# First modulation: shift and scale of the first eight k-tiles together on TensorE, without GpSimd

## The chip, the cores and the metric

The kernel runs on one core of a Trainium2 chip. The metric is the device time of one execution in microseconds (us); lower is better. Each kernel is run several times, and its median counts. One execution was also taken by the hardware profiler, and all rows below come from that one.

## What is computed

Two transformer blocks on 256 tokens of width 2048 in float32. The part at issue is the very start of the first block: a modulation of the latent `x` and of the context `ctx`, each by its own condition, and the projection of both to keys and values.

```python
def modulation(cond, w, b, n):
    m = jax.nn.silu(cond) @ w[:, :n * D_MODEL] + b[:n * D_MODEL]
    return jnp.split(m, n, axis=-1)
...
        sh, sc, gt = modulation(c_lat, w_ada[i], b_ada[i], 3)
        u = x * (1.0 + sc) + sh
...
                sh_c, sc_c = modulation(c_c, w_ada[i], b_ada[i], 2)
                uc = ctx_s * (1.0 + sc_c) + sh_c
                s_f, s_b = context_states(uc @ w_in_e[j][:, :E_STATE_COLS], w_gate_f[j], b_gate_f[j],
                                          w_gate_b[j], b_gate_b[j])
```

`w_ada[0]` is 2048 x 6144: its first 2048 columns give the shift, the next 2048 the scale. Both conditions (latent and context) meet the same weights, so the product has two rows only. Element k of shift and scale is needed before column k of `x` can enter the product `u @ w_in_e`.

## The kernel before

**Split products.** Every large product is done in three passes. `load_w` (line 157) brings two k-tiles of weights, 128 x 2 x 512 floats or 512 KB, into a buffer `wr` (four of them) by a DMA from the SP queue. `split_w` casts them to `wh` on ScalarE (line 148; three buffers) and subtracts, `wl = wr - wh`, one k-tile at a time (line 154; three buffers) on the engines of `split_on`: at first `(V, G)`, so that the first k-tile goes to VectorE and the second to GpSimd, from part 2 on `(V, V)`. `mm3` (lines 163 to 165) then does `wh*xh`, `wl*xh` and `wh*xl`. The `wr` buffer is free when the subtraction has read it.

**Modulation.** The 16 k-tiles of shift and scale are made in five parts, `PARTS = ((0, 2), (2, 2), (4, 4), (8, 4), (12, 4))` (first k-tile, count). The shift of a part (`ada_block`, kind 0) is made on TensorE: its weights go through `wr`, `wh`, `wl` like all others, and `c4`, the split condition with only four columns, is the stationary operand (lines 325 and 326). The four rows are copied (line 329), turned and summed by small products with `sel4` (line 332) and added to the bias in `mod0` (line 337). The scale of a part (`ada_block_v`, kind 1) is made on VectorE: its weights come into buffers `ar` (two of 256 KB), and each piece is multiplied by a column of the condition and added to `am`, once for the latent and once for the context (line 353 for the first, line 355 for the rest); products with a column of ones (line 361) sum over the partitions.

**Stages.** (A) The keys and values of the cross attention (`project(memT, ...)`, two blocks of 512 columns, eight steps each); beside it, in the background iterator `bg`, modulation part 0. (B) For each part j: transposes of `x` and `ctx` (line 234), scale and shift (`store_affine`, lines 249 to 252), and the products with `w_in_e` in four blocks of 512 columns, for two tiles of tokens of the latent and two of the context; beside it, in `bg`, modulation part j + 1. Part 0 leaves its sums in `kl`, `kc`, `vl`, `vc` by a copy on ScalarE (line 528). Later parts add to them: on VectorE straight from the accumulator (line 534), but for the odd tiles of tokens in parts 1 and 2 by a copy to `part` on ScalarE (line 531) and an addition on GpSimd (line 532).

**Order.** The engines run their queues in order. A scheduler of the framework sets the order of each queue from the program; work of `bg` can be moved ahead of where it is written when its buffers are free. DMAs go out from the SP queue in order, too: one that waits for its buffer holds up all behind it.

Of the kernel before, what the change touches and what calls it, by code (L numbers as in the profile page):

```python
# [17 lines left out]
D = 2048  # L18
# [36 lines left out]
def tile_kernel(ctx: ExitStack, tc: tile.TileContext, I: dict, out: bass.AP):  # L55
# [87 lines left out]
    split_on = [(V, G)]  # L143
# [26 lines left out]
    class XT:  # L170
        """x transposed, in two parts: pieces of four k-tiles, [128, 4, 256] each."""
# [10 lines left out]
    def project(x, w, c0, ncols, evac, korder=None, cw=512, w_k0=0, cbs=None, feed=None, lead=2, late=0, early=0):  # L182
        """evac(cb, t, acc) for each block of columns and each tile of tokens; feed makes x, two k-tiles at a step.
        late: the first tile of tokens is finished so many steps before the second, in the last block;
        early: the second is begun so many steps after the first, in the first block."""
# [43 lines left out]
    # transposes of two k-tiles for all tokens: src(t, kt) gives [128 tokens, 128]  # L229
# [13 lines left out]
    def store_affine(x, kt, pt, scale, bias, ts=(0, 1), scratch="h"):  # L243
        """scale(kt), bias(kt): columns [128, 1]."""
# [9 lines left out]
    def affine_steps(x, src, scale, bias, scratch="h"):  # L254
        """x from src, two k-tiles at a step; the first four k-tiles tile by tile of tokens."""
        for ts, kts in (((0,), (0, 2)), ((1,), (0, 2)), ((0, 1), range(4, 16, 2))):
            for kt in kts:
                store_affine(x, kt, transpose2(src, kt, ts), scale, bias, ts, scratch)
                yield

    # (v * scale + eps)^-1/2: a first guess from the bits, then Newton; v: [128, n]
# [22 lines left out]
    # the same for one column: a first guess by log and exp, of v * 2^-46 to stay in the log's range, then Newton  # L284
# [28 lines left out]
    mod0 = const([128, 16, 2, 2], "mod0")       # k-tile, (shift, 1 + scale), (latent, context)  # L313
    mod1 = const([128, 2, 16], "mod1")          # layer 1: (shift, 1 + scale), k-tile
    ada = [I["w_ada"][l] for l in range(2)]

    def ada_block(t0, nt, kind):
        """columns of modulation for the k-tiles t0 to t0 + nt, latent and context, on the tensor engine."""
# [15 lines left out]

    def set_mod0(pm, t0, nt, kind):
# [4 lines left out]
    def ada_block_v(t0, nt, kind):  # L340
        """the same on the vector engine."""
# [1494 lines left out]
```

## Time and profile before

| | |
|---|---|
| median of 3 runs | 2662.31 us (2661.46 to 2678.67) |
| profiled execution, its span | 2664.4 us, 2.1 us above that median |
| TensorE (PE) busy | 2522.0 us, 95% of the span |
| VectorE (DVE) busy | 1814.0 us, 68% |
| ScalarE (ACT) busy | 1164.6 us, 44% |
| GpSimd (POOL) busy | 260.0 us, 10% |
| DMA | 483.20 MB, 181 GB/s over the span |

The span runs from the first to the last instruction of the profiled execution. An engine's busy time counts its instructions, not what it waits. For TensorE it is modelled from pipelined products and says more than the product count: where a stage is dense, its products start 0.23 us apart though each shows 0.39 us. PEclk is the granted TensorE clock as a share of 2.4 GHz. A time "idle before" names what ended a wait.

### The profile page before, as it was taken

The page shows a single profiled execution, that of the slowest core. Times are in us where ns is not written, and L with a number is a line of the kernel's source. Part 1 is how long each engine was busy: PE and PEld are TensorE (multiplying, and loading weights), DVE is VectorE, ACT ScalarE, POOL GpSimd, SP SyncE. Part 2 cuts the span into 40 slices and gives each one's busy share as a digit, 9 for nine tenths or more (in the row PEclk, how much of TensorE's full clock was granted, in tenths as well). Part 3 has the DMA queues.
Part 4 walks back from the last instruction along what each step waited for, and adds up shares of the span by engine and source line. Part 5 has one row for each costly group of instructions (what it writes and reads, how often), then busy time and mean ns, then how long its engine had stood idle before and what let it go on. Part 6 is the DMA issues. An engine that isn't in the chain of part 4 may idle for free.

```text
span 2664.4 us, 33688 instructions
## 1 busy us (share of the span) xinstructions
PE 2522.0 (95%) x12095; PEld 2046.6 (77%) x12095; DVE 1814.0 (68%) x2960; ACT 1164.6 (44%) x1552; POOL 260.0 (10%) x213
## 2 busy tenths in 40 slices
PE   7889999889889899998999999999999999999998
PEld 5667866778677777787789778878788888888886
DVE  6799757897997877768656776675655544455544
ACT  5433244444654544436512352254554433444433
POOL 4430000220230000002010110100000000000000
PEclk9989999999999999999969999999999999999999
DMA  7767647667657777755512342135456555666664
GB/s 237 243 217 229 209 141 241 201 226 244 194 182 237 238 257 259 245 188 164 164 37 73 96 135 72 53 110 191 154 172 187 183 189 188 187 186 182 203 187 154
DMA packets 263012, 483.20 MB, mean 181 GB/s; under 512 B 20881, under 2 KB 37099, under 8 KB 262843
## 3 DMA queue, kind: packets, MB, share of 16 engines
q1 hardware_dynamic: 262523, 480.60, 57.6%
q8 instruction: 95, 1.56, 0.2%
q14 instruction: 74, 0.61, 0.1%
q10 hardware_dynamic: 320, 0.44, 0.0%
HBM read 477.82 MB, written 3.15 MB: 181 GB/s over the span
## 4 chain that ended last, share of the span: by engine, by line
PE 57%; DVE 7%; DMA 3%; ACT 1%; issue 1%; POOL 0%; SPq 0%; ACTq 0%; DVEq 0%; POOLq 0%
PE acc L163 16%; PE acc L165 16%; PE acc L164 16%; DMA ar<-in_w_ada 2%; DVE wl L154 2%; PE trp L234 1%; PE pzc L1355 1%; PE pwc L1361 1%; PE pw L1381 1%; PE pz L1375 1%; DVE aa L379 1%; PE psr L1329 0%; ACT wh L148 0%; DVE w L1344 0%; DMA lng<-in_ln_g 0%
## 5 line engine op out<-in xcount | busy, mean ns | idle before, releaser
L148 ACT CAST wh<-wr 128x1024 fp32r<-128x1024 f32 (+2 forms) x720 | 743.7, 1038 | 1044.5 <-PE acc L165 866.5
L164 PE MATMUL acc<-wl,xh 128*128 128x512 f32 (+2 forms) x2688 | 1067.5, 397 | 32.5 <-DVE wl L154 32.2
L163 PE MATMUL acc<-wh,xh 128*128 128x512 f32 (+2 forms) x2688 | 1073.8, 401 | 14.1 <-ACT xh L251 6.0
L165 PE MATMUL acc<-wh,xl 128*128 128x512 f32 (+2 forms) x2688 | 1066.5, 398 | 2.2 <-DVE xl L252 2.2
L154 DVE TENSOR_TENSOR wl<-wr,wh 128x512 fp32r<-128x512 f32 (+3 forms) x864 | 584.0, 704 | 171.4 <-ACT wh L148 170.2
L164 PEld LDWEIGHTS acc<-wl,xh 128*128 128x128 f32 x2688 | 516.5, 192 | 151.1 <-DVE wl L154 45.9
L163 PEld LDWEIGHTS acc<-wh,xh 128*128 128x128 f32 x2688 | 515.7, 192 | 131.0 <-ACT wh L148 8.1
L165 PEld LDWEIGHTS acc<-wh,xl 128*128 128x128 f32 x2688 | 516.3, 192 | 112.1 <-DVE xl L252 4.0
L151 DVE TENSOR_TENSOR wl<-wr,wh 128x1024 fp32r<-128x1024 f32 x272 | 333.2, 1225 | 357.4 <-ACT wh L148 355.4
L379 DVE SCALAR_TENSOR_TENSOR aa<-ar,cs,aa 128x512 f32<-128x512 f32 x240 | 192.0, 800 | 76.4 <-DMA ar<-in_w_ada 74.4
L355 DVE SCALAR_TENSOR_TENSOR am<-ar,cs,am 128x512 f32<-128x512 f32 (+1 forms) x150 | 109.5, 775 | 7.6 <-DMA ar<-in_w_ada 7.5
L154 POOL TENSOR_TENSOR wl<-wr,wh 128x512 fp32r<-128x512 f32 (+1 forms) x48 | 65.9, 1389 | 71.3 <-ACT wh L148 54.0
L163 PE MATMUL acc<-wh,uch 128*128 128x512 f32 x128 | 50.2, 393 | 2.5 <-DVE kc L534 2.5
L165 PE MATMUL acc<-wh,ucl 128*128 128x512 f32 x128 | 50.8, 397 | 0.0
L164 PE MATMUL acc<-wl,uch 128*128 128x512 f32 x128 | 50.8, 397 | 0.0
L1355 PEld LDWEIGHTS pzc<-xc,nd 128*128 128x128 f32 x256 | 37.0, 224 | 9.1 <-issue 8.2
L1355 PE MATMUL pzc<-xc,nd 128*128 128x32 f32 x256 | 36.6, 299 | 6.9 <-DVE xc L1352 6.9
L1361 PEld LDWEIGHTS pwc<-wc,ztc 128*128 128x128 f32 x256 | 39.3, 226 | 1.1
L701 PE MATMUL pp<-eq,ek 128*128 128x128 f32 x224 | 31.2, 294 | 8.5 <-DVE ek L713 8.5
L701 PEld LDWEIGHTS pp<-eq,ek 128*128 128x128 f32 x224 | 30.5, 209 | 11.1 <-issue 8.2
L1361 PE MATMUL pwc<-wc,ztc 128*128 128x32 f32 x256 | 37.7, 296 | 0.0
L1357 DVE TENSOR_TENSOR ztc<-pzc,lev 128x512 f32<-128x512 f32 x32 | 22.1, 692 | 21.8 <-PE pzc L1355 21.8
(568 smaller groups left out, 2408.1 us busy)
## 6 DMA issues: line engine op xcount, KB each, us to landing
ar<-in_w_ada SPq DMA_DIRECT2D x320, 256.0 KB
wr<-in_w_in_e SPq DMA_DIRECT2D x128, 512.0 KB
wr<-in_w_up SPq DMA_DIRECT2D x128, 512.0 KB
wr<-in_w_down SPq DMA_DIRECT2D x128, 512.0 KB
wr<-in_w_in SPq DMA_DIRECT2D x80, 512.0 KB
wr<-in_w_in_o SPq DMA_DIRECT2D x64, 512.0 KB
wr<-in_w_ada SPq DMA_DIRECT2D x32, 512.0 KB
wr<-in_w_out_e SPq DMA_DIRECT2D x32, 512.0 KB
```

The costliest lines, as they stand in the source:

```text
L148: S.copy(wh, wr)
L151: engines[0].tensor_tensor(wl, wr, wh.bitcast(F), op=AL.subtract)
L154: engines[q % 2].tensor_tensor(wl[:, q], wr[:, q], wh[:, q].bitcast(F), op=AL.subtract)
L163: PE.matmul(acc, xh, wh, start=start, stop=False)
L164: PE.matmul(acc, xh, wl, start=False, stop=False)
L165: PE.matmul(acc, xl, wh, start=False, stop=stop)
L234: PE.transpose(pt[:, q, t * 128:(t + 1) * 128], src(t, kt + q), ident)
L355: V.scalar_tensor_tensor(acc[a], w[:, q], col, acc[a], op0=AL.mult, op1=AL.add)
L379: V.scalar_tensor_tensor(acc, w, cs[:, k:k + 1], acc, op0=AL.mult, op1=AL.add)
L701: PE.matmul(pp[:, h, t], kx[:, 2 * h + c, s * 128:(s + 1) * 128], qx[:, 2 * h + c, t * 128:(t + 1) * 128], start=c == 0, stop=c == 1)
L1355: PE.matmul(pz[:, i], nd[:, i], xc[:, i], start=True, stop=True)
L1361: PE.matmul(pw[:, i], zt[:, i], wc[:, i], start=True, stop=True)
```

## The change

`ada_both(t0)` makes shift and scale of two k-tiles in one product on TensorE: 256 columns of shift and 256 of scale come by two DMAs of 256 KB into one `wr` buffer, are split, and meet `c4` in products of 512 columns. `ada_both(0)` takes the place of part 0 of both old functions, `ada_both(2)` of part 1, and `ada_both(4)` followed by `ada_both(6)` of part 2. Parts 3 and 4 are made as before. `split_on` is `(V, V)` from the start, and all additions to the sums in parts 1 and 2 are done on VectorE. The background takes 2, 4, 1, 1, 2 steps per step of the five parts, where it took 2, 2, 1, 1, 2. The products with `sel4` are widened to 128 columns by reading `sel4` 64 times.

```diff
-    split_on = [(V, G)]
+    split_on = [(V, V)]
...
+    def ada_both(t0):
+        acc = pbg([4, 512], "ada")
+        for k0 in range(0, 16, 2):
+            wr = sb.tile([128, 2, 512], F, name="wr", tag="wr", bufs=4)
+            for kind in range(2):
+                c0 = kind * D + t0 * 128
+                nc.sync.dma_start(wr[:, :, kind * 256:kind * 256 + 256],
+                                  ada[0][k0 * 128:(k0 + 2) * 128, c0:c0 + 256].rearrange("(k p) m -> p k m", p=128))
+            wh, wl = split_w(wr, 2, 512)
+            for q in range(2):
+                PE.matmul(acc, c4[:, k0 + q], wh[:, q], start=k0 + q == 0, stop=False)
+                PE.matmul(acc, c4[:, k0 + q], wl[:, q], start=False, stop=k0 + q == 15)
+            yield
+        m4 = tl("h", [4, 512], name="m4")
+        V.tensor_copy(m4, acc)
+        pm = pside([128, 4, 64, 2], name="pm")
+        for q in range(4):
+            PE.matmul(pm[:, q], m4[:, q * 128:(q + 1) * 128], sel4[:, None, :].to_broadcast([4, 64, 2]), start=True, stop=True)
+        for kind in range(2):
...
-    bg[0] = together(ada_block_v(*PARTS[0], 1), ada_block(*PARTS[0], 0), mem_scale())
+    bg[0] = together(ada_both(0), mem_scale())
...
-        if j == 2:
-            split_on[0] = (V, V)
...
-        bg[0] = gt_mod() if last else together(ada_block_v(*PARTS[j + 1], 1), ada_block(*PARTS[j + 1], 0))
+        bg[0] = (gt_mod() if last else together(ada_block_v(*PARTS[j + 1], 1), ada_block(*PARTS[j + 1], 0)) if j > 1
+                 else chain(*[ada_both(PARTS[j + 1][0] + q) for q in range(0, PARTS[j + 1][1], 2)]))
...
-                step(2 if last or nt == 2 else 1)
+                step((2, 4, 1, 1, 2)[j])
...
-                elif t % 2 and j < 3:
-                    part = tl("h", name="part")
-                    S.copy(part, acc[t])
-                    G.tensor_tensor(dst, part, dst, op=AL.add)
```

The queues change at the front only: from the middle of part 4 on, every engine has the same instructions in the same order as before. Three places show how. First VectorE in the first column block of stage A, before (`xl` belongs to the transposed memory tokens, `am` to the scale, `wl` is a weight split, 128x512 for the cross weights and 128x256 for the shift):

```order
L154 TENSOR_TENSOR wl<-wr,wh 128x512
L431 SCALAR_TENSOR_TENSOR xl<-trp,pr_77,xh 128x256 x2
L355 SCALAR_TENSOR_TENSOR am<-ar,cs,am 128x256 x4
L154 TENSOR_TENSOR wl<-wr,wh 128x256 x2
L154 TENSOR_TENSOR wl<-wr,wh 128x512
L355 SCALAR_TENSOR_TENSOR am<-ar,cs,am 128x256 x4
L154 TENSOR_TENSOR wl<-wr,wh 128x256 x2
L355 SCALAR_TENSOR_TENSOR am<-ar,cs,am 128x256
```

and the same place after the change:

```order
L154 TENSOR_TENSOR wl<-wr,wh 128x512 x3
L455 SCALAR_TENSOR_TENSOR xl<-trp,pr_77,xh 128x256 x3
L154 TENSOR_TENSOR wl<-wr,wh 128x512 x2
L455 SCALAR_TENSOR_TENSOR xl<-trp,pr_77,xh 128x256 x2
L154 TENSOR_TENSOR wl<-wr,wh 128x512 x8
```

The splits no longer stand behind scale work; there are more of them. Second, VectorE in the middle of part 0, before (`am` 128x256 is the scale of part 1, `am` 128x512 of part 2, `m` the copy of line 329):

```order
L355 SCALAR_TENSOR_TENSOR am<-ar,cs,am 128x256 x7
L154 TENSOR_TENSOR wl<-wr,wh 128x256 x2
L355 SCALAR_TENSOR_TENSOR am<-ar,cs,am 128x256 x5
L353 TENSOR_SCALAR am<-ar,cs 128x512
L154 TENSOR_TENSOR wl<-wr,wh 128x512
L329 COPY m_943<-ada 4x256
L154 TENSOR_TENSOR wl<-wr,wh 128x512
```

and after, where line 379 is the old line 355 and its `am` the scale of part 3:

```order
L379 SCALAR_TENSOR_TENSOR am<-ar,cs,am 128x512
L154 TENSOR_TENSOR wl<-wr,wh 128x512 x2
L379 SCALAR_TENSOR_TENSOR am<-ar,cs,am 128x512 x4
L154 TENSOR_TENSOR wl<-wr,wh 128x512 x6
L379 SCALAR_TENSOR_TENSOR am<-ar,cs,am 128x512 x4
L154 TENSOR_TENSOR wl<-wr,wh 128x512 x6
L379 SCALAR_TENSOR_TENSOR am<-ar,cs,am 128x512 x4
```

The scale of part 3, which stood in part 2 before, has moved forward into stage A and parts 0 and 1: all 32 of its instructions stand ahead of the first evacuation of part 2. Third, the SP queue in part 1, before:

```order
L159 DMA wr<-in_w_in_e 128x2x512
L347 DMA ar<-in_w_ada 128x512 x2
L159 DMA wr<-in_w_ada 128x2x512 x2
L347 DMA ar<-in_w_ada 128x512 x2
L159 DMA wr<-in_w_in_e 128x2x512
L347 DMA ar<-in_w_ada 128x512
L159 DMA wr<-in_w_ada 128x2x512
L347 DMA ar<-in_w_ada 128x512
```

and after, where line 342 is the pair of DMAs of `ada_both`:

```order
L371 DMA ar<-in_w_ada 128x512
L342 DMA wr<-in_w_ada 128x2x256 x2
L159 DMA wr<-in_w_in_e 128x2x512
L342 DMA wr<-in_w_ada 128x2x256 x8
L159 DMA wr<-in_w_in_e 128x2x512
L342 DMA wr<-in_w_ada 128x2x256 x8
L159 DMA wr<-in_w_in_e 128x2x512
```

Between two loads of `w_in_e` there are now four `wr` loads of modulation weights in eight DMAs, where there were two `wr` loads and some `ar` loads.

## Rows read from the trace of the kernel before

**Rows 1.** The page: span, and busy time of each engine.

```profile
span 2664.4 us, 33688 instructions
...
PE 2522.0 (95%) x12095; PEld 2046.6 (77%) x12095; DVE 1814.0 (68%) x2960; ACT 1164.6 (44%) x1552; POOL 260.0 (10%) x213
```

**Rows 2.** Windows: length, busy PE, PEld, DVE, ACT, POOL (counts), PEclk, DMA, GB/s.

```profile
17.50:80.00 62.50, 57.52 (x253) 44.24 (x254) 47.55 (x92) 31.15 (x46) 35.34 (x27) 0.95 0.73 239
80.00:87.90 7.90, 3.63 (x24) 2.15 (x23) 7.90 (x18) 4.05 (x7) 2.26 (x3) 0.89 0.84 253
87.90:119.10 31.20, 27.48 (x118) 21.35 (x118) 22.18 (x36) 14.94 (x23) 11.78 (x9) 0.92 0.76 242
119.10:165.00 45.90, 35.90 (x145) 24.33 (x144) 40.85 (x45) 17.64 (x24) 26.97 (x18) 0.89 0.65 208
165.00:171.25 6.25, 6.25 (x43) 5.93 (x41) 4.20 (x9) 3.73 (x7) 0.54 (x1) 0.75 0.43 138
171.25:223.40 52.15, 51.77 (x225) 38.89 (x224) 51.74 (x79) 20.95 (x28) 10.51 (x7) 1.00 0.80 255
```

**Rows 3.** Waits of PE from 17.5 to 165: us in total, times, longest.

```profile
PE acc L164 <- DVE wl L154: 12.5, 7, 3.7
PE ada L326 <- DVE wl L154: 6.5, 6, 3.1
PE acc L163 <- DVE kc L534: 2.5, 1, 2.5
```

**Rows 4.** Groups of DVE from 17 to 168, shapes apart: busy us, mean ns.

```profile
L355 DVE SCALAR_TENSOR_TENSOR am<-ar,cs,am 128x256 f32<-128x256 f32 x60 | 34.9, 630 | 1.7 <-DMA ar<-in_w_ada 1.7
L355 DVE SCALAR_TENSOR_TENSOR am<-ar,cs,am 128x512 f32<-128x512 f32 x30 | 29.7, 1027 | 5.9 <-DMA ar<-in_w_ada 5.7
L154 DVE TENSOR_TENSOR wl<-wr,wh 128x512 fp32r<-128x512 f32 x34 | 28.6, 846 | 9.3 <-ACT wh L148 9.1
L154 DVE TENSOR_TENSOR wl<-wr,wh 128x256 fp32r<-128x256 f32 x16 | 9.9, 652 | 0.0
```

**Rows 5.** The same from 229 to 289, where GpSimd does nothing.

```profile
L154 DVE TENSOR_TENSOR wl<-wr,wh 128x512 fp32r<-128x512 f32 x33 | 21.5, 685 | 0.6 <-ACT wh L148 0.3
L355 DVE SCALAR_TENSOR_TENSOR am<-ar,cs,am 128x512 f32<-128x512 f32 x28 | 19.7, 747 | 0.0
```

**Rows 6.** Groups of POOL from 0 to 229 (three more like the last).

```profile
L154 POOL TENSOR_TENSOR wl<-wr,wh 128x512 fp32r<-128x512 f32 x32 | 52.2, 1641 | 60.6 <-ACT wh L148 43.3 <-DMA wr<-in_w_ada 15.3 <-DMA xn<-in_ctx 2.0
L154 POOL TENSOR_TENSOR wl<-wr,wh 128x256 fp32r<-128x256 f32 x16 | 13.9, 885 | 10.7 <-ACT wh L148 10.7
L532 POOL TENSOR_TENSOR kl<-part,kl 128x512 f32<-128x512 f32 x4 | 6.6, 1638 | 26.5 <-ACT part L531 26.5
```

**Rows 7.** Line 534: duration in ns, least, median, most; first and last start.

```profile
L534 DVE TENSOR_TENSOR kl<-acc,kl x12: 679/684/692, 129.8 to 313.8; 128x512 f32<-128x512 f32 x12
```

**Rows 8.** Timeline of DVE in part 0: start, us, instruction, idle before.

```profile
104.67 1.00 DVE L353 TENSOR_SCALAR am<-ar,cs 128x512 f32<-128x512 f32 x1 [4.08 <-DMA ar<-in_w_ada]
105.59 0.68 DVE L154 TENSOR_TENSOR wl<-wr,wh 128x512 fp32r<-128x512 f32 x1
```

**Rows 9.** Timeline of PE behind that wait.

```profile
106.32 0.56 PE L164 MATMUL acc<-wl,xh 128*128 128x512 f32 x1 [3.72 <-DVE wl L154]
...
107.10 0.63 PE L163 MATMUL acc<-wh,xh 128*128 128x512 f32 x1
...
110.31 0.39 PE L164 MATMUL acc<-wl,uch 128*128 128x512 f32 x1
```

**Rows 10.** Timeline of the SP queue: issues of the fifth and sixth cross-weight loads.

```profile
30.81 0.37 SPq L159 DMA_DIRECT2D wr<-in_w_kv_cross  x1
...
34.17 0.37 SPq L159 DMA_DIRECT2D wr<-in_w_kv_cross  x1
```

**Rows 11.** Timeline of ACT: the casts of those two loads.

```profile
36.17 1.05 ACT L148 CAST wh<-wr 128x1024 fp32r<-128x1024 f32 x1 [0.19 <-DMA wr<-in_w_kv_cross]
38.91 1.05 ACT L148 CAST wh<-wr 128x1024 fp32r<-128x1024 f32 x1 [1.70 <-DMA wr<-in_w_kv_cross]
```

More of the change, by code (lines that the diff above doesn't have):

```diff
@@ L333, in ada_block @@
         set_mod0(pm, t0, nt, kind)
+    def ada_both(t0):
[17 more added lines that the diff above has]
+        for kind in range(2):
+            b = pr1[:, 32 + kind * 16 + t0:32 + kind * 16 + t0 + 2]
+            V.scalar_tensor_tensor(mod0[:, t0:t0 + 2, kind, :], pm[:, 2 * kind:2 * kind + 2, 0, :], float(kind),
+                                   b[:, :, None].to_broadcast([128, 2, 2]), op0=AL.add, op1=AL.add)
     def set_mod0(pm, t0, nt, kind):
```

## Prediction

> **What bounds the kernel now.** TensorE is busy 95% of the span and sets the end [rows 1], so a change at the front counts as far as it lets TensorE's queue advance earlier. I read the windows by stage first: stage A runs from 17.5 to 80.0, its passage to part 0 to 87.9, part 0 to 119.1, part 1 to 165.0, its passage to part 2 to 171.25, and part 2 to 223.4 [rows 2]. The reader should compare part 2 with the rest. In part 2, 192 products with `w_in_e` and 32 of modulation (225 rows) take 52.15 us, 0.232 us each, at full clock: dense, though VectorE is busy 51.74 of the 52.15 us. Ahead of it TensorE is idle 5.0, 4.3, 3.7 and 10.0 us in four stretches, at a mean clock of 0.89 to 0.95 of 2.4 GHz. Priced at 0.232 us per 512-column product and half of that for a 256-column one (an estimate), the work of A is 192 x 0.232 + 32 x 0.116 + about 3 for transposes = 51 of 62.5 us; of part 0 about 25 of 31.2; of part 1 about 30 of 45.9. So some 37 us are lost between 17.5 and 165, and only there can the change win.
>
> Who is late is read from the waits: 12.5 us for `wl` in the main products, 6.5 us for `wl` in the modulation products, 2.5 us at once for an evacuation on line 534; all are VectorE [rows 3]. A wait costs more than itself: after 3.72 us of idleness the products last 0.63 us at 107.10 and 0.39 us again only at 110.31 [rows 9], the lower of the two clock levels (1.2 GHz) for about 3.5 us, some 1.6 us lost. That wait itself began at VectorE: a scale instruction stood 4.08 us for its `ar` transfer, and the split that TensorE needed stood behind it [rows 8].
>
> Why is VectorE late in the front and not in part 2? Its instructions stretch there. A split of 512 columns takes 846 ns and a scale step 1027 ns on the mean [rows 4], against 685 and 747 ns where GpSimd is silent [rows 5]. GpSimd does 48 splits and 16 additions there, 52.2 + 13.9 + 4 x about 6 us [rows 6]. Line 534, whose first operand comes from the accumulator, never stretches: 679 to 692 ns [rows 7]. The Trainium skill, SBUF — State Buffer, "Who interferes with whom", says that GpSimd and a VectorE instruction with two SBUF inputs take one port pair as an exclusive lock and the second waits for the first. The rows agree with it on who is hit; taken as a price it would make the whole 90 us of GpSimd a loss, while the excess of the groups in [rows 4] over the quiet means is 30 x 0.28 + 34 x 0.16 + 60 x about 0.2 + 16 x about 0.2, near 30 us. The sum below uses neither figure, only quiet durations.
>
> **Part by part.**
> *Removed.* 90 scale steps and their six first ones from VectorE: 34.9 + 29.7 us and about 3 [rows 4]. The 48 splits and 16 additions on GpSimd, and with them the stretching. Sixteen copies to `part` on ScalarE, which is busy 31.15 of 62.5 us at most [rows 2]: covered.
> *Added on VectorE.* GpSimd's splits, 32 x 0.685 + 16 x about 0.41 = 28.5 us; splits of the scale weights, 16 loads x 2 x 0.685 = 21.9 us; 16 evacuations x 0.684 = 10.9 us, 8 of them in part 2 [rows 5, 7]. 61.3 against 67.5 us: alone this is almost even. Then the scheduler pulls all 32 scale steps of part 3 forward, 22 us more. So VectorE gets no lighter in the front; what it loses is the stretching and the bad order, splits behind long runs of scale work.
> *Added on TensorE.* Modulation products: 32 of 512 columns instead of 256 for part 0 (in A) and again for part 1 (in part 0), 32 more for part 2 (in part 1): 3.7 + 3.7 + 7.4 = 14.8 us. The column sums of line 361 go; the widened ones come; I call that even.
> *Added on ScalarE.* 16 casts x 1.05 us [rows 11] against the 16 copies: hidden.
> *Moved on SP and DMA.* Bytes are the same, but the `ar` loads of part 3 (16 x 0.262 = 4.2 MB) come ahead of part 2. Counted from the order, 14 cross loads, 30 modulation loads and 9 of `w_in_e` (53 x 0.524 MB), the `ar` loads, inputs and stores make about 36 MB between 17.5 us and part 2. Each `wr` load of modulation is two issues of 0.37 us [rows 10]; SP mostly waits for buffers, so these are free.
>
> Now the stages, against the profiled execution.
> Stage A: TensorE's floor is 192 x 0.232 + 32 x 0.232 + 3 = 55; VectorE needs 48 splits and about 20 other steps, at the 0.655 us per instruction of part 2 (51.74 / 79) [rows 2] some 45 us: not the bound. With 1.5 us for filling the buffers, 56.5: **-6** (bounds -7.5 and 0).
> Passage to part 0: scale and shift of `x` waited for stretched scale steps; now two splits and one step stand ahead. **-3.5** of 7.9 (bounds -5 and 0).
> Part 0: TensorE 96 + 25 products x 0.232 plus 0.5 = 28.5; VectorE 24 splits + 14 scale steps x 0.655 + 3 for the inputs = 28; transfers 12 x 0.524 + 8 x 0.262 + 1.5 = 9.9 MB, of which about 1.6 come early, 32.5 us at the 255 GB/s of part 2. All are near each other, so between 28.5 and 35; I take 31.7: **+0.5**.
> Part 1: TensorE 160 x 0.232 + 1.4 = 38.5; VectorE 40 splits + 16 evacuations + 5 scale steps x 0.655 + 3.6 = 43.5, the bound: **-2.5** (bounds -7.5 and +8). Here the 8 evacuations taken from GpSimd count in full.
> Passage to part 2, and later parts: part 2 has 8 evacuations more on VectorE (5.2 us) but some ten scale steps fewer (6.5) and no stretching (32 x 0.09 us and less); TensorE is dense there already. **-0.5** (bounds -2 and +1.5).
> Sum -12.0. As a cross-check, 36 MB at 255 GB/s take 141 us where 153.75 were used: -13. Nothing behind takes it back: from part 4 on all queues read the same. The profiled execution is 2664.4 us, 2.1 above the median of the runs; 2662.3 - 12 = **2650 us**.
>
> **Rivals.**
> *TensorE's floor.* If every stall goes, A 55, passage 3, part 0 28.5, part 1 38.5, passage 6: 131 against 153.75, -23: 2639. For it: the products are dense in part 2 with VectorE at 99%. Against: in part 1 VectorE's sum is 5 us above TensorE's.
> *Transfers stay slow.* The stretch from 17.5 to 171.25 moved 34.9 MB at 227 GB/s [rows 2]. At the 239 of stage A, 36 MB take 150.6 us: -3, 2659. For it: the front was short of transfers too (5.7 us of waits for `ar` in one group [rows 4]), and `ar` work stands between splits again. Against: those 227 GB/s hold windows in which the queue waited for buffers that VectorE held.
> *Slower: the four `wr` buffers.* All modulation weights of three parts go through `wr` now. 53 loads on 4 buffers are 13.25 trips each; with trips of 11.6 us the front is as long as before. From issue to cast a load took 5.4 and 4.7 us [rows 10, 11]; cast, two splits and issue make it 7.6 us, so 4 us of queueing in every trip decide. At 12.2 us the front takes 161.7: +8, 2670. Against: VectorE would have to leave a landed load lying for 4 us each time, as it did only around the waits for `ar`.
>
> **How the numbers follow.** The forecast (2643 to 2656) gets 0.58, TensorE's floor 0.17, slow transfers 0.17, the buffers 0.08. The range 2635 to 2664 takes in the first three with their edges and leaves out the buffers and some tails, under 0.2. One per cent, about what a measurement of this kernel can tell from no change, is 26.6 us: faster than 2635.7 only beyond TensorE's floor, 0.06; slower than 2689 only with trips far over 12 us, 0.02; within, 0.92.
>
> **What the profile after would show.** GpSimd empty from 3 us to part 4. Splits at 685 ns also in the front. Stage A's last product at about 74 us, part 0's first main product near 78, part 2's near 159. PE waiting in part 1 for splits and line 534, a few us. If part 1 is as long as before, VectorE's sum or the transfers were the bound; if waits name `wr` transfers, the buffers. The forecast is wrong if losses of the front remain though VectorE is quiet, or if the 12 us come back behind part 2.

## The result, and the profile after

The kernel after the change takes 2659.98 us in the median of 20 runs (2614.75 to 2691.30), the kernel before beside it 2678.70 (20 runs, 2652.64 to 2697.08). The ratio is 0.9882, with a 95% interval of 0.9841 to 0.9922: 1.2% faster by this measure. The ratio compares the runs of each kernel near its own fastest, and as two runs of the new kernel came out at 2614.75 and 2621.09 us, its upper group (above 2655) fell out of that comparison and most of the upper group of before did not. The medians are 18.7 us apart. In a second set of runs of the same two kernels (e9) the medians are 2668.3 after (12 runs) and 2667.6 before (23 runs), so they show no gain there. Over all runs of this study the mean is 2658.8 us after (32 runs) and 2671.7 before (108 runs), 12.9 us apart with an uncertainty of 7 (twice the joint standard error of 3.2 and 1.6).

The profiled execution after has a span of 2662.0 us, 2.4 us less than the one before (2664.4), though its front is 11 us shorter. Both facts have to be explained: the 11 us, and where they are at the end.

The page after, its span and busy times, to be set beside [rows 1]; GpSimd (POOL) falls from 260.0 to 171.7 us:

```profile
span 2662.0 us, 33655 instructions
...
PE 2542.2 (95%) x12111; PEld 2062.5 (77%) x12111; DVE 1783.0 (67%) x2947; ACT 1171.7 (44%) x1552; POOL 171.7 (6%) x149
```

The same six stages of the kernel after by windows, which answer to [rows 2]: stage A, its passage to part 0, part 0, part 1, its passage to part 2, part 2. Columns: length, busy PE, PEld, DVE, ACT, POOL (counts), PEclk, DMA, GB/s:

```profile
17.40:74.72 57.32, 57.29 (x248) 42.94 (x249) 42.27 (x84) 35.25 (x50) 0.00 (x0) 1.00 0.85 278
74.72:82.28 7.56, 3.31 (x17) 1.41 (x16) 6.41 (x11) 3.51 (x6) 0.00 (x0) 0.88 0.83 273
82.28:115.02 32.74, 31.65 (x130) 22.30 (x129) 23.74 (x38) 20.82 (x29) 0.00 (x0) 0.92 0.79 257
115.02:155.90 40.88, 40.55 (x177) 24.50 (x176) 39.20 (x69) 20.17 (x23) 0.00 (x0) 1.00 0.84 272
155.90:162.31 6.41, 5.61 (x32) 4.20 (x31) 4.95 (x12) 4.49 (x7) 0.00 (x0) 0.74 0.88 304
162.31:213.24 50.93, 50.93 (x221) 38.70 (x222) 45.11 (x73) 16.29 (x18) 0.00 (x0) 1.00 0.72 231
```

Stage A is 5.2 us shorter, part 1 5.0, part 2 1.2. The passage to part 0 is nearly as long as before (7.56 us against 7.90), part 0 is 1.5 us longer. Part 2 starts 8.9 us earlier (162.31 against 171.25), part 4 11.4 us (281.01 against 292.42).

VectorE's two large groups after, from 17 to 162 us, which answer to [rows 4]: busy us, mean ns, idle before:

```profile
L154 DVE TENSOR_TENSOR wl<-wr,wh 128x512 fp32r<-128x512 f32 x117 | 74.5, 687 | 17.0 <-ACT wh L148 16.8
L379 DVE SCALAR_TENSOR_TENSOR am<-ar,cs,am 128x512 f32<-128x512 f32 x29 | 20.7, 748 | 5.8 <-DMA ar<-in_w_ada 5.8
```

Splits and scale steps now last in the front what they lasted before only where GpSimd was silent [rows 5]: 687 instead of 846 ns, 748 instead of 1027. TensorE's waits from 17.4 to 162.3 us, which answer to [rows 3]:

```profile
PE ada L347 <- DVE wl L154: 4.5, 3, 2.7
PE pm L353 <- DVE m L350: 1.9, 2, 1.1
PE acc L163 <- ACT wh L148: 0.6, 1, 0.6
```

The 12.5 us of waits for `wl` in the main products and the waits on line 534 are gone. What is left stands in the passage to part 0. VectorE's timeline there (start, us, instruction, idle before) shows scale steps of part 3, moved far ahead, that wait for their transfers with splits behind them:

```profile
77.29 0.75 DVE L379 SCALAR_TENSOR_TENSOR am<-ar,cs,am 128x512 f32<-128x512 f32 x1 [0.93 <-DMA ar<-in_w_ada]
77.95 1.29 DVE L154 TENSOR_TENSOR wl<-wr,wh 128x512 fp32r<-128x512 f32 x2
79.16 0.75 DVE L379 SCALAR_TENSOR_TENSOR am<-ar,cs,am 128x512 f32<-128x512 f32 x1
79.82 0.99 DVE L249 TENSOR_SCALAR full<-trp,mod 128x256 f32<-128x256 f32 x2
```

TensorE's timeline in the same place waits twice for those splits, and part 0 then begins with products of 0.63 us, the lower level of the clock (1.2 GHz), as behind the wait in [rows 9]:

```profile
78.69 0.39 PE L347 MATMUL ada<-wl,c 128*4 128x512 f32 x1 [2.71 <-DVE wl L154]
...
81.46 0.59 PE L347 MATMUL ada<-wl,c 128*4 128x512 f32 x1 [1.54 <-DVE wl L154]
...
82.28 0.63 PE L163 MATMUL acc<-wh,xh 128*128 128x512 f32 x1
```

**Where the 11 us went in this pair of profiles.** From the middle of part 4 on the queues are the same. The first product of line 1374 in the new kernel (the inverses of small triangular matrices in the second mixer; line 1355 in the old one) comes at 1335.4 us, before the change at 1357.4. That is 22.0 us earlier: 11.4 from the front, and 10.6 between the start of part 4 and the inverses, where the two kernels are all but the same. This second stretch lasts 1053.9 to 1065.0 us over all profiles of this study, and 1054.4, 1055.0 and 1060.6 in the three of the kernel after, so the 10.6 us can be scatter; their cause was not sought. The stretch from there to the last such product has the same instructions in both. First the kernel before, then the one after, by windows:

```profile
1357.40:1695.40 338.00, 325.95 (x2060) 286.44 (x2061) 222.11 (x514) 107.05 (x170) 30.63 (x32) 0.91 0.29 85
```

```profile
1335.40:1695.70 360.30, 348.31 (x2060) 308.17 (x2061) 220.37 (x514) 106.86 (x170) 31.41 (x32) 0.85 0.27 80
```

The work is the same, but the granted clock is 0.85 instead of 0.91 and the stretch 22 us longer: it takes back all that was ahead. Behind it the new kernel gains 2.7 us more, which leaves the 2.4. Within the stretch the trace before has one long piece at 1.2 GHz (41 us from 1359), the trace after two (44 us each, from 1337 and from 1412). In such a piece TensorE counts as busy all the time and gets through about half as many products per us: the first row is 40 us of the kernel after at the lower level, 179 products; the second, of the kernel before, 20 us of such work at the upper, 167 products.

```profile
1340.00:1380.00 40.00, 40.00 (x179) 39.95 (x179) 13.95 (x35) 4.02 (x6) 0.00 (x0) 0.50 0.14 39
```

```profile
1440.00:1460.00 20.00, 20.00 (x167) 19.88 (x166) 12.64 (x29) 4.28 (x6) 0.00 (x0) 1.00 0.46 134
```

Whether that is the change's doing or chance is a question for the experiments (e9, e11).

### The profile page after: what moved, and what is told of

Its sections match the earlier page's. It is cut to its first block, busy times and chain, and to the rows that moved or that the text cites. A ratio compares the mean times of both kernels' runs of the same rounds, so it can differ in the third digit from the quotient of the medians.

```text
span 2662.0 us, 33655 instructions
## 1 busy us (share of the span) xinstructions
PE 2542.2 (95%) x12111; PEld 2062.5 (77%) x12111; DVE 1783.0 (67%) x2947; ACT 1171.7 (44%) x1552; POOL 171.7 (6%) x149
## 4 chain that ended last, share of the span: by engine, by line
PE 58%; DVE 7%; DMA 3%; ACT 1%; issue 1%; POOL 0%; SPq 0%; ACTq 0%; DVEq 0%; POOLq 0%
PE acc L163 16%; PE acc L165 16%; PE acc L164 16%; DMA ar<-in_w_ada 3%; PE trp L234 1%; PE pzc L1374 1%; PE pwc L1380 1%; DVE wl L154 1%; DVE aa L403 1%; PE pw L1400 1%; PE pz L1394 1%; ACT wh L148 1%; PE psr L1348 0%; DVE w L1363 0%; DMA lnb<-in_ln_b 0%
## 5 line engine op out<-in xcount | busy, mean ns | idle before, releaser
L148 ACT CAST wh<-wr 128x1024 fp32r<-128x1024 f32 (+2 forms) x736 | 760.1, 1038 | 1083.9 <-PE acc L165 890.7
L154 DVE TENSOR_TENSOR wl<-wr,wh 128x512 fp32r<-128x512 f32 (+2 forms) x928 | 616.7, 697 | 197.1 <-ACT wh L148 196.2
L1374 PEld LDWEIGHTS pzc<-xc,nd 128*128 128x128 f32 x256 | 43.1, 255 | 8.5 <-issue 6.1
L379 DVE SCALAR_TENSOR_TENSOR am<-ar,cs,am 128x512 f32<-128x512 f32 x60 | 42.8, 748 | 8.5 <-DMA ar<-in_w_ada 8.5
L1380 PEld LDWEIGHTS pwc<-wc,ztc 128*128 128x128 f32 x256 | 46.3, 262 | 1.1
L1380 PE MATMUL pwc<-wc,ztc 128*128 128x32 f32 x256 | 44.0, 326 | 0.0
L1381 DVE TENSOR_TENSOR wc<-pwc,wc 128x128 f32<-128x128 f32 x32 | 9.3, 292 | 43.0 <-PE pwc L1380 43.0
```

The lines of the kernel that those rows point to most:

```text
L148: S.copy(wh, wr)
L154: engines[q % 2].tensor_tensor(wl[:, q], wr[:, q], wh[:, q].bitcast(F), op=AL.subtract)
L379: V.scalar_tensor_tensor(acc[a], w[:, q], col, acc[a], op0=AL.mult, op1=AL.add)
L1374: PE.matmul(pz[:, i], nd[:, i], xc[:, i], start=True, stop=True)
L1380: PE.matmul(pw[:, i], zt[:, i], wc[:, i], start=True, stop=True)
```

## The experiments

The theory (S): VectorE's stretching beside GpSimd and the order behind it cost the front its time, and GpSimd's leaving gives it back. The rival (M): the scale work that leaves VectorE does it. Since the timed runs scatter by 20 us in steps, the kernels are compared above all by marks: the start of the first main product of parts 0, 1, 2 and 4 in each profile. The times stand beside them; they are too coarse to rank the versions (e1 and e5, with the same marks, have medians 17 us apart).

The ratio of e1 to e12, formed as in the result above, is to the runs of the kernel before beside them, whose medians were 2671.2 (e1 to e4), 2675.7 (e5 to e8) and 2667.6 (e9 to e12).

| run | part 0 | part 1 | part 2 | part 4 | median us (runs) | ratio to before, 95% |
|---|---|---|---|---|---|---|
| before | 87.9 | 123.5 | 171.2 | 292.4 | 2678.7 (20) | |
| after | 82.3 | 118.6 | 162.3 | 281.0 | 2660.0 (20) | 0.988 (0.984 to 0.992) |
| e1 no GpSimd | 79.7 | 109.1 | 152.8 | 272.5 | 2646.9 (12) | 0.991 (0.987 to 0.994) |
| e2 both, GpSimd back | 86.7 | 132.5 | 199.6 | 313.9 | 2687.6 (12) | 1.003 (0.998 to 1.008) |
| e3 after + GpSimd load | 95.2 | 139.8 | 201.9 | 316.1 | 2684.7 (11) | 1.010 (1.007 to 1.014) |
| e4 scale behind part 0 | 77.2 | 113.4 | 156.7 | 274.5 | 2662.9 (12) | 1.000 (0.995 to 1.005) |
| e5 only splits off GpSimd | 80.2 | 109.6 | 153.2 | 273.5 | 2664.1 (10) | 1.003 (0.998 to 1.008) |
| e6 scale behind part 1 | 77.7 | 111.4 | 155.8 | 270.8 | 2656.4 (10) | 1.001 (0.996 to 1.006) |
| e7 e1 + products twice | 78.7 | 112.6 | 157.3 | 277.8 | 2661.0 (10) | 0.995 (0.990 to 1.000) |
| e8 e1 + parts early | 78.1 | 105.8 | 153.3 | 287.7 | 2664.5 (10) | 0.998 (0.991 to 1.006) |
| e9 after again | 81.7 | 116.9 | 160.6 | 279.7 | 2668.3 (12) | 0.995 (0.991 to 1.000) |
| e10 mix | 79.2 | 108.4 | 152.3 | 269.9 | 2652.4 (12) | 0.991 (0.987 to 0.995) |
| e11 after, wide | 82.8 | 118.2 | 161.8 | 280.6 | 2622.0 (6) | 0.982 (0.977 to 0.986) |
| e12 mix, wide | 80.3 | 109.5 | 152.7 | 269.6 | 2612.0 (6) | 0.977 (0.973 to 0.982) |

The kernel after stands in it three times with the same front (after, e9, e11): its marks lie within 1.8 us of each other, the one at part 4 within 1.3. The marks before come from one profile.

### e1: GpSimd out, scale left on VectorE

```diff
-    split_on = [(V, G)]
+    split_on = [(V, V)]
...
-                elif t % 2 and j < 3:      # copy to part, addition on GpSimd
+                elif t % 2 and j < 0:
```

> The kernel before with GpSimd taken out of the front alone: all splits on VectorE from the start, all additions to the sums in parts 1 and 2 on VectorE, scale still made on VectorE. Theory S (what the front loses is VectorE's stretching beside GpSimd, and the order behind it): VectorE takes on about 28 + 11 us of instructions and gets back about 30 us of stretching, so the front stays about as long: first main product of part 2 at 168 to 174 us (171.25 before, 162.31 after the change), splits at 685 to 700 ns. Theory M (the gain comes from the scale work that leaves VectorE, GpSimd is beside the point): VectorE, with 40 us more in a front where it is the late one, pushes part 2 back by 10 us or more, to 181 to 200, and the time to 10 to 30 us above before.

Part 2 starts at 152.8 us, 18.5 earlier than before and 9.5 earlier than after the change; part 4 19.9 and 8.5 earlier. M is refuted: VectorE has more to do and the front is shorter. S had the direction of the stretching right and missed the mark by 15 us (it gave 168 to 174): half of the change does more than all of it. Stage A with its passage, part 0 with its passage, part 1 with its passage, by windows:

```profile
17.50:79.70 62.20, 58.12 (x273) 44.73 (x274) 55.80 (x140) 35.06 (x52) 0.00 (x0) 1.00 0.88 284
79.70:109.10 29.40, 29.30 (x145) 22.17 (x144) 24.74 (x51) 19.04 (x29) 0.00 (x0) 1.00 0.85 282
109.10:152.80 43.70, 38.17 (x163) 27.66 (x161) 38.96 (x65) 13.92 (x17) 0.00 (x0) 0.89 0.65 203
```

VectorE keeps the scale work and is still below the length of each stage. Its groups show that the instructions of [rows 4] are short without GpSimd, the narrow ones too (630 to 480 ns, 652 to 420):

```profile
L355 DVE SCALAR_TENSOR_TENSOR am<-ar,cs,am 128x256 f32<-128x256 f32 x60 | 25.7, 480 | 3.5 <-DMA ar<-in_w_ada 3.5
L355 DVE SCALAR_TENSOR_TENSOR am<-ar,cs,am 128x512 f32<-128x512 f32 x30 | 20.7, 746 | 3.0 <-DMA ar<-in_w_ada 3.0
L154 DVE TENSOR_TENSOR wl<-wr,wh 128x256 fp32r<-128x256 f32 x32 | 11.4, 420 | 0.0
```

### e2: shift and scale together on TensorE, GpSimd put back

```diff
 # after the change, and:
+    split_on = [(V, G)]       # until part 2
...
+                elif t % 2 and j < 3:
+                    S.copy(part, acc[t])
+                    G.tensor_tensor(dst, part, dst, op=AL.add)
```

> The kernel after the change, with GpSimd put back: second split of every pair on GpSimd until part 2, additions of the odd tiles of tokens in parts 1 and 2 on GpSimd through a copy. Theory S: splits on VectorE stretch to 780 to 850 ns again (687 after the change), GpSimd's own splits take about 1.1 us and are late by themselves, and part 2 starts at 166 to 172 us: half of the 9 us or more are gone. Theory M (moving the scale products does it): part 2 starts at 160 to 164 us and the first product of part 4 at 279 to 283, as after the change, whatever the splits last.

Both theories were wrong on the size. Part 2 starts at 199.6 us, 28 later than before the change; part 4 21.5 later. The wide loads put one 512-column split on GpSimd for every one on VectorE, and VectorE's largest groups (17 to 200 us) stretch more than in any other run here:

```profile
L154 DVE TENSOR_TENSOR wl<-wr,wh 128x512 fp32r<-128x512 f32 x61 | 62.7, 1038 | 27.5 <-ACT wh L148 22.4 <-ACT kc L553 5.0
L379 DVE SCALAR_TENSOR_TENSOR am<-ar,cs,am 128x512 f32<-128x512 f32 x40 | 42.8, 1092 | 14.5 <-DMA ar<-in_w_ada 14.5
```

The half that gives the change its name is a loss beside GpSimd. Why it also costs 8.5 us without GpSimd (e1 against after) is asked in e4, e6 and e7.

### e3: the price of GpSimd alone

```diff
 # after the change, and behind each cast of 512 columns until part 2:
+            G.tensor_copy(noise[0][:, 0:1], wh[:, 0, 0:1].bitcast(F))
+            G.tensor_tensor(noise[0], cst[:, 0:512], cst[:, 128:640], op=AL.add)
```

> The kernel after the change, with one addition of 512 columns on GpSimd, of constants into a tile that nobody reads, behind each cast of a pair of k-tiles until part 2 (some 56 of them, nothing left out of the computation). It prices the stretching alone. Theory S: splits on VectorE last 750 to 830 ns instead of 687 and part 2 starts 4 to 8 us later than after the change, at 166 to 170 us. Rival (TensorE is the bound in the front now and hides it): splits stretch but part 2 starts within 1.5 us of 162.3.

Part 2 starts at 201.9 us, 39.6 later than after the change: far beyond S, and the rival falls. No split and no sum uses a result of this work. The splits and scale steps on VectorE, then the work on GpSimd, from 17 to 202 us:

```profile
L156 DVE TENSOR_TENSOR wl<-wr,wh 128x512 fp32r<-128x512 f32 x117 | 104.2, 938 | 7.8 <-ACT wh L150 6.6 <-ACT kc L559 1.3
...
L384 DVE SCALAR_TENSOR_TENSOR am<-ar,cs,am 128x512 f32<-128x512 f32 x30 | 27.7, 958 | 6.3 <-DMA ar<-in_w_ada 6.3
```

```profile
L159 POOL TENSOR_TENSOR noise<-cst 128x512 f32<-128x512 f32 x56 | 91.6, 1636 | 4.5
L158 POOL COPY noise<-wh 128x1 f32<-128x1 f32 x56 | 27.9, 498 | 62.2 <-ACT wh L150 60.0
```

117 x 0.251 + 30 x 0.210 is 36 us of stretching in these two groups, for 91.6 us of additions and 27.9 us of copies on GpSimd. The front loses 39.6. This is not the price of stretching alone: each copy reads one column of `wh`, so a buffer of `wh` is free for the next cast only when GpSimd has come to it, and ScalarE waits for that 8.0 us in all. TensorE's long waits name VectorE, 29.3 us in three groups, and the casts 0.9 us, so the stretching should be the larger part; how the 39.6 us divide was not measured. The waits from 17 to 202 us (us in total, times, longest):

```profile
PE ada L352 <- DVE wl L156: 12.9, 7, 3.4
PE acc L169 <- DVE wl L156: 10.1, 11, 1.5
...
PE pm L358 <- DVE m L355: 6.3, 3, 5.3
...
ACT wh L150 <- POOL noise L159: 5.2, 3, 2.6
...
ACT wh L150 <- POOL noise L158: 2.8, 1, 2.8
```

### e4 and e6: when the scale of part 3 runs

```diff
 # after the change, and:
-        ... together(ada_block_v(*PARTS[j + 1], 1), ...
+        ... together(behind(anchor, ada_block_v(*PARTS[j + 1], 1)) ...   # for part 3
 # anchor: VectorE's last step of scale and shift of x, of part 0 (e4) or of part 1 (e6)
```

> The kernel after the change, with the scale steps of part 3 queued on VectorE behind the last scale and shift of part 0, so that none stands in stage A or in the passage to part 0. Theory H (the passage stayed at 7.6 us, where 4.4 was forecast, because scale steps moved ahead wait for their transfers there with splits and the affine steps behind them): the passage shrinks to 4 to 5 us, part 2 starts at 158 to 160.5 us, the first product of part 4 is 2 to 4 us earlier than 281.0. Rival (the passage is the chain from the last modulation product over copies, small products and transposes, at the lower clock): the passage stays at 7 to 8 us and part 2 starts at 161.5 to 164.

H holds, and the gains are larger than it said. TensorE's timeline of e4: the last product of stage A ends, transposes, modulation of part 1, and the first product of part 0 comes 3.4 us later, at full clock; the passage took 7.6 in the kernel after:

```profile
73.82 1.04 PE L234 MATMUL trp<-cst,xn 128*128 128x128 f32 x8
...
76.42 0.39 PE L347 MATMUL ada<-wl,c 128*4 128x512 f32 x1 [0.34 <-DVE wl L154]
...
77.25 0.39 PE L163 MATMUL acc<-wh,xh 128*128 128x512 f32 x1
```

Part 2 starts 5.6 us earlier than after the change, part 4 6.5. But part 0 with its passage stays at 36.2 us, where e1 has 29.4. That is what e6 asks:

> The kernel after the change, with the scale steps of part 3 queued on VectorE behind the last scale and shift of part 1, so that none stands in stage A, in part 0 or in the passages to parts 0 and 1. With the anchor at part 0 the first products of parts 0, 1, 2 and 4 came at 77.2, 113.4, 156.7 and 274.5 us; part 0 with its passage stayed at 36.2 us, against 29.4 in the kernel before without GpSimd. Theory P (part 0 is bound by TensorE, which got 32 products of 512 columns there instead of 32 of 256): part 0 stays at 35 to 36.5 us, part 1 loses 0 to 2 us, part 2 gains what VectorE gets there, part 4 at 273 to 278. Theory Q (the scale weights of part 3 and their steps hold up part 0): part 0 shrinks to 30 to 32 us, part 1 begins at 107 to 109.

Part 0 falls to 33.7 us, neither the 35 to 36.5 of P nor the 30 to 32 of Q: the scale steps of part 3 explain 2.5 of the 6.8 us. VectorE is then busy 18.2 of the 33.7 us and TensorE 32.4, at full clock, so what remains is TensorE's:

```profile
77.70:111.40 33.70, 32.39 (x146) 21.98 (x146) 18.24 (x32) 22.98 (x33) 0.00 (x0) 1.00 0.68 208
```

### e5: splits or additions

```diff
 # before the change, and:
-    split_on = [(V, G)]
+    split_on = [(V, V)]
```

> The kernel before with the splits alone taken off GpSimd; its 16 additions to the sums in parts 1 and 2 stay there, and scale stays on VectorE. It divides the gain of the run without GpSimd (first products of parts 0, 1, 2 and 4 at 79.7, 109.1, 152.8 and 272.5 us, against 87.9, 123.5, 171.2 and 292.4 before). Theory S1 (the 48 splits cost the front its time, late by themselves and stretching VectorE; the additions cost little): 79 to 81, 108 to 111, 151 to 156 and 271 to 277. Theory S2 (additions of GpSimd stretch VectorE as much per us): the first two are as in S1, but part 1 is 4 us longer or more, part 2 at 157 or later and part 4 at 278 or later.

S1: the marks are those of e1 within 1 us. The 16 additions on GpSimd cost next to nothing, though VectorE's scale steps beside them still stretch (864 ns on the mean from 109 to 215 us, 748 in part 2 of e1): stretched instructions alone do not make the front late. The 48 splits cost 19 us.

### e7: TensorE's share

```diff
 # e1, and in ada_block for parts 0 to 2:
+                    PE.matmul(acc, zero4, wh[:, q], start=False, stop=False)
+                    PE.matmul(acc, zero4, wl[:, q], start=False, stop=False)
```

> The kernel before without GpSimd, with each modulation product of parts 0 to 2 followed by one of the same weights with a stationary operand of zeros, so that TensorE has as many columns of modulation as after the change (an estimate of 3.7, 3.7 and 7.4 us in stage A, part 0 and part 1), and VectorE, ScalarE and the transfers have what they had; the sums don't change. Theory P (what the change costs on its own, 281.0 against 272.5 at the first product of part 4, is TensorE's time): part 0 at 82 to 84, part 0 with its passage 32 to 34, part 1 at 43 to 47, part 4 at 278 to 284. Rival (it is the wide loads, casts and splits in VectorE's and ScalarE's queues, and TensorE has room): part 4 at 271 to 275.

Part 4 starts at 277.8 us, 5.2 later than in e1, just below P's 278 to 284. In stage A the added products cost nothing (part 0 at 78.7, where P had 82 to 84), in part 0 4.5 us, 33.9 as in e6, where TensorE does as many columns; part 1 is 1.0 us longer. TensorE's time alone is thus worth some 5 us. But the 8.5 us between e1 and the change hang on the scale steps of part 3, pulled ahead: e6, which sends them back and keeps the move to TensorE, has part 4 at 270.8, 1.8 us earlier than e1. It loses 5.0 us to e1 in parts 0 and 1 and gets them back in stage A and parts 2 and 3. So the move is a loss in the order that the scheduler gave it, and with the scale steps behind part 1 it costs nothing at part 4.

### e8: parts early, a version that lost

```diff
 # e1, and:
+            if cb == 3 and not last:
+                drain()
+                feed_part(j + 1)    # loads, transposes, scale and shift of the next part
...
-                step(2 if last or nt == 2 else 1)
+                step((3, 3, 2, 2, 2)[j])
```

> A version meant to beat both: the kernel before without GpSimd, with the background taking 3, 3, 2, 2, 2 steps, so that a part's modulation is ready before the last block of columns of the part ahead, and with the loads, transposes, scale and shift of the next part written ahead of that last block. Theory V1 (the passages of 6 to 10 us between parts are a chain of modulation, transposes, scale and shift that TensorE waits for): parts 1 to 3 shrink from 43.7, 60.3 and 59.4 us to 39 to 42, 53 to 57 and 53 to 57, and part 4 starts at 256 to 266 us (272.5 without this edit). Theory V2 (VectorE is the bound there, busy 39.0 of 43.7 and 55 of 60 us, and only pays in another order): part 4 starts at 269 to 275 us.

Neither: part 4 starts at 287.7 us, 15 later than in e1. Part 0 gains 1.7 us, but each later part is longer: part 1 by 3.8 us, part 3 by 3.3, and part 2 with its passage takes 71.7 instead of 60.3. VectorE is busy 65.3 us of it, where e1 has 55.3: it does 39 scale steps and 36 splits there instead of 30 and 32, so part of the work of part 3 has been pulled ahead. That this is the whole loss was not tested.

### e9: the kernel after once more

> The kernel after the change once more, unchanged: how far the marks of a stage move from one profiled execution to the next. If the marks tell the kernels apart, the first products of parts 0, 1, 2 and 4 come within 1 us of 82.3, 118.6, 162.3 and 281.0; if they move by 4 us or more, the small differences between the runs above show nothing. The number of long stretches at 1.2 GHz between 1330 and 1720 us (two in the profile after, one in the one before, 15 to 22 us each) is taken for chance: it should differ from run to run of the same kernel, in groups of times about 20 us apart.

The marks repeat, within 1.8 us (above), not quite the 1 us expected. And the stretch of the inverses is another: one long piece at 1.2 GHz (44 us from 1392) where the profile after had two, 335.3 us instead of 360.3 for the same work, and the whole execution took 2640.8 us instead of 2663.8:

```profile
1334.70:1670.00 335.30, 324.27 (x2060) 285.04 (x2061) 221.38 (x513) 106.94 (x171) 33.42 (x32) 0.92 0.29 86
```

The 12 timed runs lie at 2640.8 to 2649.9 (five), 2667.8 to 2678.2 (four) and 2687.3 to 2691.0 (three). So the number of long pieces differs between executions of one program; the difference in the pair of profiles above by itself says nothing of the change. All twelve profiles with the products of 32 columns have one to three such pieces.

### e10: the mix

```diff
 # after the change, and:
-    bg[0] = together(ada_both(0), mem_scale())
+    bg[0] = together(ada_block_v(*PARTS[0], 1), ada_block(*PARTS[0], 0), mem_scale())
 # part 1 by ada_block_v and ada_block, too; part 2 by ada_both;
 # scale of part 1 behind VectorE's last step for x of part 0, of part 3 behind that of part 1
```

> What the stages so far point to, put together: GpSimd out of the front, shift on TensorE and scale on VectorE for parts 0 and 1 as before the change, shift and scale of part 2 together on TensorE as after it, and the scale steps of parts 1 and 3 queued on VectorE behind the scale and shift of x of the part ahead. From the best stage lengths seen (60 to 62, 29.4, 43.7, 57.4, 57.6 us): first products of parts 0, 1, 2 and 4 at 78 to 80, 107 to 109, 151 to 153 and 265 to 269 us. Rival: the stages are not independent, what VectorE is spared in one it has to do in the next; then part 4 starts at 270 to 274, as without GpSimd (272.5) and with the late scale (270.8).

Part 4 starts at 269.9 us (269.6 in e12), 2.6 earlier than e1 and 0.9 than e6 (the latter within the scatter of the marks): just outside the forecast of 265 to 269, and nearer to the rival. Part 2 did not add up as hoped (60.4 us, 57.4 in e6); the other stages came near the lengths that were put together.

### e11 and e12: wide products in the inverses

```diff
-                    PE.matmul(pz[:, i], nd[:, i], xc[:, i], start=True, stop=True)
+                    PE.matmul(pz[:, i], nd[:, i], xc[:, i, None, :].to_broadcast([128, 4, 32]), ...)
 # line 1380 likewise; VectorE reads the wide result, or its first quarter
```

> The kernel after the change, with the products of 32 columns in the triangular inverses of the second mixer (lines 1374 and 1380) widened to 128 columns by reading the operand four times; VectorE's steps read the wide result or its first quarter, and the sums are the same. It asks why the profile after shows nothing of the 11 us of the front at its end. Theory C (a stage of small products with waits between them falls to 1.2 GHz in some executions and stays there for 41 to 48 us at 15 to 22 us each, and more columns keep the clock): no stretch at the lower level over 20 us between 1330 and 1720, times within 10 us of each other, at 2610 to 2630. Rival (the widened products cost as much as the clock gives): median at 2645 to 2670, as after the change, or above.

C holds: no long piece is left, the clock over the stretch is 0.99, and it takes 299.2 us (with 1981 products instead of 2060: fewer of the large products fall into the shorter stretch):

```profile
1341.20:1640.40 299.20, 288.70 (x1981) 250.60 (x1982) 216.52 (x501) 99.47 (x163) 33.33 (x32) 0.99 0.29 85
```

The six runs lie between 2620.0 and 2629.8 us, and the median is 46 us below that of the same kernel without the edit, run beside it (e9, 2668.3). The wide products are not dearer: line 1374 in e9, then in e11 (the count is the same). The means mix both levels of the clock; the medians, 276 and 275 ns, are alike:

```profile
L1374 PE MATMUL pzc<-xc,nd 128*128 128x32 f32 x256 | 36.2, 298 | 5.2 <-DVE xc L1371 5.2
```

```profile
L1374 PE MATMUL pzc<-xc,nd 128*128 128x128 f32 x256 | 33.1, 280 | 5.7 <-DVE xc L1371 5.7
```

> The mix of the run above and the widened products together: the version that should beat both kernels. If both theories hold, 2595 to 2615 us at one level; if only the mix holds, groups of times 20 us apart from about 2605 up; if only the widening holds, as the kernel after with widened products, within 3 us.

2612.0 us (2604.2 to 2616.4), a ratio of 0.977 to before: the best version of the study. It stands 10.0 us below e11, and its front is 11.0 us ahead at part 4. With the long pieces gone, a gain of the front is seen about whole at the end, as far as six runs of each, spread over 10 and 12 us, can tell. The kernel before with wide products was not run, so the change itself has no such clean pair.

## Why the prediction was right, and where not

The time is in the range; the forecast of 2650 was 10 us too low against the median of 20 runs, which stands beside a before of 2678.7 and not 2662.3. By the difference, -12 was forecast; the front shows -11.4 at part 4, -12.7 in e9; the means of all runs are 12.9 apart, the medians 18.7, the ratio says about 32 (0.0118 x 2678.7). The first three agree with the forecast. That the time fell into the range was in part luck: with the before of 2678.7 a gain of 12 would have ended at 2667, above it, and the second median of the same kernel (e9, 2668.3) lies above it, too. So was the agreement of the sum: the table shows a passage 3.2 us worse and a part 1 2.5 us better than forecast, which nearly cancel. The chance of 0.06 for more than 1% rested on times that repeat; the median of the kernel before was 2662.3 us in its first three runs and 2667.6 to 2678.7 in the larger sets, and a ratio with a narrow interval moved from 0.988 to 0.995 for the same program (e9).

*Term by term, to part 4.*

| term | forecast | profile after |
|---|---|---|
| stage A | -6 | -5.2 |
| passage to part 0 | -3.5 | -0.3 |
| part 0 | +0.5 | +1.5 |
| part 1 | -2.5 | -5.0 |
| passage to part 2, and later | -0.5 | +0.2, then -1.2 and -1.2 |

*The stretching.* The cause was right: e1 and e5 show it by taking GpSimd's splits away, and e3 by putting in GpSimd work that nobody needs. e1 and e5 by themselves leave open whether GpSimd's splits, at 1641 ns each [rows 6], were simply late. Against it, TensorE's waits before name VectorE's splits and none of GpSimd's [rows 3]; ScalarE's casts wait for GpSimd's splits 4.0 us in all. The size was taken too small. The prediction called the exchange on VectorE "almost even" and left the merit with the stretching, but gave the move to TensorE no price as a whole. e1 and e2 have it: without the move the front is 8.5 us shorter, and with the move and GpSimd 21.5 us longer than before; e6 shows that the 8.5 us hang on the order of the scale steps of part 3.

The Trainium skill, SBUF — State Buffer, "Who interferes with whom", says that a VectorE instruction with two SBUF inputs contends with a GpSimd instruction that reads SBUF. e3 agrees on who is hit: its additions share no data with the splits, which last 938 ns beside them and 687 without. The stretching comes to 36 us in e3, for 119.5 us of GpSimd.

*The passage to part 0* is the step that failed: "now two splits and one step stand ahead". The order showed 32 scale steps of part 3 pulled forward, and the prediction counted them in VectorE's sum and not in this passage, where they wait for transfers. e4 takes them away, and the passage is 3.4 us (4.4 was forecast): that step cost the forecast 3.2 us of its 3.5.

*Part 0.* The largest of its three terms was the transfers at 255 GB/s; the stage moved 257 GB/s, which looks like agreement. But e6 has the same kind of part 0 at 208 GB/s and 33.7 us, and e1 282 GB/s and 29.4. TensorE's products set most of it: e7 adds nothing but products and lengthens it by 4.5 us (3.7 was the estimate); the scale steps of part 3 add 2.5 (e4 against e6). That the passage of 29.4 us is so short in e1 has another reason that only was read, not tested: its modulation products of part 1 fill the time in which `x` is made ready.

*Part 1* was sized by VectorE's sum at the 0.655 us per instruction of part 2, which GpSimd still stretched, though the prediction says that it uses only quiet durations; after, it is 39.20 / 69 = 0.568 in part 1 and 45.11 / 73 = 0.618 in part 2, so the mix of instructions counts as well. VectorE was not the bound that it was taken for: TensorE is busy 40.55 of the 40.88 us, at full clock, one product every 0.231 us.

*The rivals.* TensorE's floor, 131 us for the four stages and passages to part 2: after 144.9, e1 135.3, so it was nearer than thought for the half of the change. The four buffers did not decide: no wait of TensorE in the front names a transfer. Nor were the transfers slow: by the windows above the front moved 39.5 MB at 272 GB/s. (The prediction's cross-check, 36 MB at 255 GB/s, was low on both, and so agreed.) What came true of that rival is its last remark, `ar` work between splits: that is the passage to part 0. "Nothing behind takes it back" was right of the queues and wrong of the pair of profiles: a second piece at half clock, which comes and goes from one execution to the next, took 22 us.

## What to carry to other kernels

When a change joins two edits, price each alone: here one brought part 4 forward by 20 us and the other, in the order that it got, put it back by 8.5, and the order of the queues alone would have shown neither. Where TensorE waits for VectorE, VectorE's two-input work beside GpSimd is dear even if GpSimd's result is not needed by anyone (938 against 687 ns in e3); look at the same instruction where the other engine is silent. Before believing a difference of 1%, see how the times of one program group, and compare marks inside the profile; a stage of small products between waits can hide or feign the whole gain, and steadying it (e11, 46 us) was worth more than the change.

## What was not expected of the hardware

Pieces of a stage in which TensorE is never idle by the profile ran at 1.2 GHz for 41 to 48 us at a time, one to three times in each profile with the narrow products. One piece more cost 22 and 25 us (360.3 us with two against 338.0 and 335.3 with one, for the same products). In the profile after it fell at 1337 us, behind 1.5 us of idleness and the first products of 32 columns, and rose again at 1381. The same products with 128 columns last no longer (medians of 275 against 276 ns) and kept the stretch at 0.98 to 0.99 of full clock in both profiles taken.
